# A segment mean on one core: looks in fewer operations, part of VectorE's work moved to GpSimd

## The chip, the cores and the metric

The kernel runs on one core of a Trainium2 chip. The metric is the device time of one execution in microseconds (us); lower is better. Each time below is the median of several executions, and the range stands beside it. The profile is one further execution, taken by the hardware profiler; its span is a little shorter than the times (193.8 us for the kernel before).

The engines: VectorE (DVE in the profile) and ScalarE (ACT) do the arithmetic, GpSimd (POOL) issues the gathers and does a little arithmetic, SyncE (SP) issues the plain loads, TensorE (PE) is hardly used. In the traces of this case each engine starts its instructions in the order in which the program records them, and stands still where something that it needs from another engine or from a DMA is not there yet (the stands below, of 6.5 and 8.4 us, are such waits).

## The reference

```python
n, num_segments = 10_000_000, 10000
data = randn(n) as float32
segment_ids = sorted random integers, int64

sums, counts = zeros(num_segments), zeros(num_segments)
np.add.at(sums, segment_ids, data)
np.add.at(counts, segment_ids, 1)
return sums / np.maximum(counts, 1)
```

The ids are sorted, and a segment has about 1000 elements. The kernel uses both facts, checks that they hold as it needs them, and has a slow general path for other inputs.

## The kernel before

Each of the 128 partitions holds 78,125 consecutive elements and goes through them in 98 rows of 800. A row of 800 is expected to hold at most one border between two segments. So the ids need not all be read:

1. *Probes.* Every 160th id is loaded. A **look** on VectorE (ten small operations for five rows) counts how many of a row's probes still equal the first one. This tells in which block of 160 the border lies.
2. *Gather.* GpSimd fetches the 159 ids at that place with an indirect DMA, one for each row.
3. *Id count.* ScalarE adds up the 159 gathered ids. VectorE turns the sums of five rows into border positions `KK` with one operation (`second_look`).
4. *Total and split.* ScalarE adds up the 800 data of the row. VectorE adds up those in front of the border, in one operation (`split`).
5. *Tables.* Now and then VectorE turns finished rows into segment counts, sums and means, puts them in order of the segments (`select`, `table`), and shifts each partition's table to its place in the output (`place`). A few checks add up flags that would call for the general path (`check`, `verdict`).

```python
def first_look(g):                       # before: 10 operations
    eq  = (probes == first probe)        # s1
    V   = first id of each row
    jc  = reduce(eq); BT = V[1:] - V     # s2
    ST  = jc * S + (1 + W)               # s3
    NB  = (BT != 1)
    pos = ST + wb                        # s4
    QQ  = V * W + ST
    IDX = NB * BIG + pos                 # s5
    QQ  = NB * (-64 * BIG) + QQ
    gather(g)                            # five indirect DMAs on GpSimd

def add_ids(r):
    nc.scalar.activation(
        out=junk_a[:, 0:W], in_=gt32[:, r % RING, 0 : 2 * W : 2], func=ACT.Relu,
        accum_out=GS[:, r : r + 1],
    )

def second_look(a, b):                   # KK = QQ - GS
    nc.vector.tensor_sub(out=KK[:, a:b], in0=QQ[:, a:b], in1=GS[:, a:b])

def split(r):                            # one operation per row on VectorE
    nc.vector.scalar_tensor_tensor(
        out=junk_v[:, 0:n], in0=iota[:, 0:n], scalar=KK[:, r : r + 1], in1=d,
        op0=ALU.is_lt, op1=ALU.mult, accum_out=A[:, r : r + 1],
    )
```

(These four are shortened; the first is in pseudo-code.) The author fixes the order of all instructions: the main loop goes row by row, and a list says which extra step is recorded behind which row. The engines' queues follow this order. The schedule of the tables before the change, with cuts:

```python
X_LOOK, X_SUM, RING = 11, 6, 28     # a look is 11 rows ahead, an id count 6 rows
for g in range(HEAD, NG):
    put(max(bounds[g] - X_LOOK, 0), first_look(g), 5)
put(45, select(0, 8, v))            # v: VectorE, g: GpSimd
put(52, sums(0, 48) + table(0, 8, v))
put(58, select(8, 12, v))
put(67, sums(48, 66) + table(8, 12, v) + place(0, 36, v), 2)
put(60, check(), 2)
# ...
for r in range(-X_PROBE - X_DATA, NR):
    # ... loads on SyncE, add_ids(r + X_SUM) on ScalarE ...
    total(r)                        # ScalarE
    split(r)                        # VectorE
    for f in after[r]:              # the steps put behind this row
        f()
```

## Time and profile before

The kernel before took 195.88 us (median of 3 runs, 195.34 to 196.23).

| engine | busy, share of the span | what it mainly does |
|---|---|---|
| VectorE | 148.1 us, 76% | 98 splits of 1.04 us, some 350 small operations (551 instructions less the splits and the reads of their sums) |
| ScalarE | 138.1 us, 71% | 98 totals of 0.87 us, 98 id counts of 0.35 us, and reading out the sums |
| GpSimd | 105.2 us, 54% | 98 gathers of 1.0 us |
| DMA | 9 tenths or more in 35 of 40 slices | 53 MB |

The page of the kernel before, part 1 (busy time, share of the span, instructions) and part 2 (busy tenths in 40 slices):

```profile
PE 1.6 (1%) x6; PEld 1.4 (1%) x6; DVE 148.1 (76%) x551; ACT 138.1 (71%) x393; POOL 105.2 (54%) x117
...
DVE  6438197868694958596788849997996778999991
ACT  0221789999987878595989679767949796977800
POOL 5487776764647383636456472757274564862000
DMA  6999999999999999999999999999999999993000
```

The DMA row is full up to slice 36, so the data stream sets the time up to about 177 us. Behind that VectorE alone stays at 9, up to slice 39: it finishes the last rows and tables. (A slice is 4.8 us.)

The groups of the kernel before (part 5 of the page: line, engine, operation, tiles, shapes, count, then busy us and mean ns, then the idle time in front and what ended most of it):

```profile
L289 POOL DMA_INDIRECT GT<-in_segment_ids_dram,IDX x98 | 98.3, 1003 | 66.7 <-ACT junk_a L299 26.0
L319 DVE SCALAR_TENSOR_TENSOR junk_v<-iota,q,data_t 128x800 bf16<-128x800 f32 x98 | 102.3, 1044 | 26.1 <-DMA data_t<-in_data_dram 24.6
...
L299 ACT ACTIVATE junk_a<-GT 128x159 bf16<-128x159 int32 x98 | 33.9, 346 | 23.6 <-DMA GT<-in_segment_ids_dram,IDX 19.5
```

VectorE's splits were idle for 26.1 us in all, of which data that had not landed ended 24.6 us. VectorE is faster than the stream and catches up with it again and again.

### The profile page before, as it was taken

Reading aid. Unit: us, or ns where it says so; the run is one execution under the profiler, and the core shown is the slowest. Engines: PE = TensorE matmul, PEld = TensorE weight load, DVE = VectorE, ACT = ScalarE, POOL = GpSimd, SP = SyncE. Lnnn points to the kernel's source line nnn. Section 1 sums busy time; section 2 is a strip of 40 time slices with the busy share of each in tenths; the row PEclk is TensorE's granted clock in tenths of the full one; section 3 lists DMA queues with packets and bytes.
Section 4 is the critical chain, followed back from the end, with each engine's and each line's share of the span. In section 5 each row is a group of like instructions: output and inputs, shape, how many; then the busy total and the mean of one; then the engine's idle time right before and its main releaser. Section 6 shows DMA issues by size and latency. Waiting matters only on the chain.

```text
span 193.8 us, 1611 instructions
## 1 busy us (share of the span) xinstructions
PE 1.6 (1%) x6; PEld 1.4 (1%) x6; DVE 148.1 (76%) x551; ACT 138.1 (71%) x393; POOL 105.2 (54%) x117
## 2 busy tenths in 40 slices
PE   0000000000000100000000000000000000001000
PEld 0000000000000100000000000000000000001000
DVE  6438197868694958596788849997996778999991
ACT  0221789999987878595989679767949796977800
POOL 5487776764647383636456472757274564862000
DMA  6999999999999999999999999999999999993000
GB/s 63 131 172 353 293 396 238 310 337 347 258 261 393 265 351 184 409 205 378 260 403 249 265 380 294 333 236 410 226 327 325 347 254 406 411 394 144 2 0 10
DMA packets 75141, 53.40 MB, mean 275 GB/s; under 512 B 65601, under 2 KB 65684, under 8 KB 75127
## 3 DMA queue, kind: packets, MB, share of 16 engines
q1 hardware_dynamic: 70251, 40.54, 74.6%
q0 software_dynamic: 4704, 12.74, 22.4%
q14 instruction: 14, 0.11, 0.2%
q10 hardware_dynamic: 172, 0.00, 0.1%
HBM read 56.46 MB, written 0.04 MB: 291 GB/s over the span
## 4 chain that ended last, share of the span: by engine, by line
DMA 37%; SPq 29%; issue 13%; DVE 13%; POOL 3%; ACT 2%; POOLq 0%; ACTq 0%; DVEq 0%
DMA data_t<-in_data_dram 31%; SPq L161 24%; DVE junk_v L319 6%; DMA GT<-in_segment_ids_dram,IDX 6%; SPq L153 5%; POOL GT L289 3%; ACT junk_a L314 1%; ACT junk_a L299 1%; DVE FF L572 1%; DVE most L706 0%; DVE add L701 0%; DVE pk L684 0%; DVE sel L628 0%; DVE sel L642 0%; DVE tab L647 0%
## 5 line engine op out<-in xcount | busy, mean ns | idle before, releaser
L289 POOL DMA_INDIRECT GT<-in_segment_ids_dram,IDX x98 | 98.3, 1003 | 66.7 <-ACT junk_a L299 26.0
L319 DVE SCALAR_TENSOR_TENSOR junk_v<-iota,q,data_t 128x800 bf16<-128x800 f32 x98 | 102.3, 1044 | 26.1 <-DMA data_t<-in_data_dram 24.6
L314 ACT ACTIVATE junk_a<-data_t 128x800 bf16<-128x800 f32 x98 | 85.0, 867 | 14.3 <-DMA data_t<-in_data_dram 11.6
L299 ACT ACTIVATE junk_a<-GT 128x159 bf16<-128x159 int32 x98 | 33.9, 346 | 23.6 <-DMA GT<-in_segment_ids_dram,IDX 19.5
L299 ACT ACTIVATION_READ_ACCUMULATOR junk_a<-GT 128x1 f32 x98 | 18.3, 186 | 0.0
L314 ACT ACTIVATION_READ_ACCUMULATOR junk_a<-data_t 128x1 f32 x98 | 18.3, 186 | 0.0
L306 DVE TENSOR_TENSOR q<-QQ,GS 128x5 f32<-128x5 f32 (+1 forms) x20 | 3.2, 160 | 8.2 <-ACT junk_a L299 8.2
L319 DVE DVE_READ_ACCUMULATOR junk_v<-iota,q,data_t 128x1 f32 x98 | 8.1, 83 | 0.0
L299 ACT ACT_TABLE_LOAD x1 | 1.3, 1283 | 7.7 <-DMA data_t<-in_data_dram 7.7
L245 DVE TENSOR_TENSOR eq<-pr 128x20 f32<-128x20 int32 (+1 forms) x20 | 3.5, 173 | 4.3 <-DMA pr<-in_segment_ids_dram 4.3
L254 DVE TENSOR_SCALAR ST<-jc 128x5 f32<-128x5 f32 (+1 forms) x20 | 3.7, 183 | 0.0
L250 DVE TENSOR_REDUCE jc<-eq 128x5 f32<-128x20 f32 (+1 forms) x20 | 3.5, 175 | 0.0
L258 DVE TENSOR_SCALAR NB<-q 128x5 f32<-128x5 f32 (+1 forms) x20 | 3.4, 168 | 0.0
L268 DVE TENSOR_TENSOR pos<-ST,wb 128x5 f32<-128x5 f32 (+1 forms) x20 | 3.3, 166 | 0.1
L275 DVE SCALAR_TENSOR_TENSOR IDX<-NB,pos 128x5 int32<-128x5 f32 (+1 forms) x20 | 3.3, 165 | 0.0
L247 DVE CAST q<-pr 128x6 f32<-128x6 int32 (+2 forms) x20 | 3.3, 164 | 0.0
L279 DVE SCALAR_TENSOR_TENSOR QQ<-NB,QQ 128x5 f32<-128x5 f32 (+1 forms) x20 | 3.2, 158 | 0.0
L269 DVE SCALAR_TENSOR_TENSOR QQ<-q,ST 128x5 f32<-128x5 f32 (+1 forms) x20 | 3.1, 157 | 0.0
L251 DVE TENSOR_TENSOR q<-q 128x5 f32<-128x5 f32 (+1 forms) x20 | 3.1, 155 | 0.0
L657 POOL TENSOR_TENSOR shf<-tab,dm 128x559 f32<-128x559 f32 x1 | 1.3, 1334 | 1.9 <-DVE tab L647 1.9
L647 DVE TENSOR_REDUCE tab<-sel 128x32 f32<-128x384 f32 (+2 forms) x3 | 1.6, 531 | 0.0
L170 DVE CAST wb<-wb_i 128x98 f32<-128x98 int32 x1 | 0.8, 783 | 1.1 <-POOL wb_i L169 1.1
(107 smaller groups left out, 41.8 us busy)
## 6 DMA issues: line engine op xcount, KB each, us to landing
data_t<-in_data_dram SPq DMA_DIRECT2D x48, 800.0 KB, 10.1
GT<-in_segment_ids_dram,IDX POOLq DMA_INDIRECT x98, 6.1
pr<-in_segment_ids_dram SPq DMA_DIRECT2D x18, 25.0 KB, 9.1
data_t<-in_data_dram SPq DMA_DIRECT2D x1, 400.0 KB
data_t<-in_data_dram SPq DMA_DIRECT2D x1, 262.5 KB, 16.7
out_dram<-OUT SPq DMA_DIRECT2D x1, 36.6 KB
pr<-in_segment_ids_dram SPq DMA_DIRECT2D x1, 21.0 KB
pr<-in_segment_ids_dram SPq DMA_DIRECT2D x1, 18.0 KB
```

Source lines behind the costliest of these rows:

```text
L153: nc.sync.dma_start(out=pr_flat[:, a:b], in_=ids_p[:, a * S : (b - 1) * S + 1 : S])
L161: nc.sync.dma_start(out=d[:, 0 : c - a], in_=data_p[:, a:c])
L245: nc.vector.tensor_tensor(out=eq, in0=in0b, in1=in1b, op=ALU.is_equal)
L247: nc.vector.tensor_copy(out=V[:, a:e], in_=pr32[:, a:e, 0])
L250: nc.vector.tensor_reduce(out=jc, in_=eq, axis=AX.X, op=ALU.add)
L254: nc.vector.tensor_scalar(out=ST[:, a:b], in0=jc, scalar1=float(S), scalar2=float(1 + W), op0=ALU.mult, op1=ALU.add,)
L258: nc.vector.tensor_scalar(out=NB[:, a:b], in0=BT[:, a:b], scalar1=1.0, scalar2=None, op0=ALU.not_equal)
L268: nc.vector.tensor_add(out=pos, in0=ST[:, a:b], in1=wb[:, a:b])
L289: nc.gpsimd.indirect_dma_start(out=GT[:, r % RING, :], out_offset=None, in_=ids2d[:], in_offset=bass.IndirectOffsetOnAxis(ap=IDX[:, r : r ...
L299: nc.scalar.activation(out=junk_a[:, 0:W], in_=gt32[:, r % RING, 0 : 2 * W : 2], func=ACT.Relu, accum_out=GS[:, r : r + 1],)
L314: nc.scalar.activation(out=junk_a[:, 0:n], in_=d, func=ACT.Copy, accum_out=t)
L319: nc.vector.scalar_tensor_tensor(out=junk_v[:, 0:n], in0=iota[:, 0:n], scalar=KK[:, r : r + 1], in1=d, op0=ALU.is_lt, op1=ALU.mult, accum_ ...
```

## The change

The intent: fewer operations on VectorE, which has no pause from 160.5 us to its end, and use of GpSimd, which is busy for 54% of the span only.

- A look takes seven operations instead of ten. The id count gets a bias of minus the row's first id for each partition, so that ScalarE's sum *is* the number of ids beyond the border, and less is left for VectorE to undo.
- Several table products, the window checks, and a new middle table move to GpSimd. The diff writes each fused operation of VectorE as two instructions of GpSimd, so a check becomes seven instructions there in place of four on VectorE.
- The counts take five steps instead of seven. Looks stand ten rows ahead instead of eleven, id counts five instead of six.

The core of the diff, with cuts:

```diff
-X_LOOK = 11
-X_SUM = 6
-RING = 28
+X_LOOK = 10
+X_SUM = 5
+RING = 20
...
     def add_ids(r):
         nc.scalar.activation(
             out=junk_a[:, 0:W], in_=gt32[:, r % RING, 0 : 2 * W : 2], func=ACT.Relu,
+            bias=NV[:, r : r + 1],
             accum_out=GS[:, r : r + 1],
         )
...
-            nc.vector.tensor_sub(out=KK[:, a:b], in0=QQ[:, a:b], in1=GS[:, a:b])
+            nc.vector.scalar_tensor_tensor(
+                out=KK[:, a:b], in0=JC[:, a:b], scalar=float(S), in1=GS[:, a:b], op0=ALU.mult, op1=ALU.subtract
+            )
...
     def windows_hold(r, n, o1, o2):
-        def s1():
-            nc.vector.scalar_tensor_tensor(
-                out=j1[:, 0:n], in0=KEY[:, PAD + r : PAD + r + n], scalar=-1.25, in1=ur[:, r : r + n],
-                op0=ALU.mult, op1=ALU.add,
-            )
+        e = nc.gpsimd
+        def s1():
+            e.tensor_scalar(
+                out=j1[:, 0:n], in0=KEY[:, PAD + r : PAD + r + n], scalar1=-1.25, scalar2=None, op0=ALU.mult
+            )
+            e.tensor_tensor(out=j1[:, 0:n], in0=j1[:, 0:n], in1=ur[:, r : r + n], op=ALU.add)
...
-    put(45, select(0, 8, v))
-    put(52, sums(0, 48) + table(0, 8, v))
-    put(58, select(8, 12, v))
-    put(67, sums(48, 66) + table(8, 12, v) + place(0, 36, v), 2)
+    put(43, select(M1, NT1 // 4, g))
+    t, p = table(M1, NT1 // 4, g, tax), place(CE, NO, tax, ...)
+    put(45, t[:1])                     # product on GpSimd
+    put(47, t[1:] + p[:1])             # its reduction on VectorE, then the place on GpSimd
+    put(44, select(0, 8, g))
+    put(58, select(8, 12, g))
+    t, p = table(8, 12, g, tab), place(0, 36, tab, ...)
+    put(69, t[:1])                     # product on GpSimd
+    put(71, t[1:] + p[:1])             # its reduction on VectorE
+    look = bounds[NG - 1] - X_LOOK
+    put(look + 3, verdict())
+    after[look + 6].append(lambda: verdict_reg.append(nc.values_load(...)))
```

The looks stand behind rows 44, 49, ... 64, 69, ..., five rows apart. So the products put behind rows 45 and 69 come into GpSimd's queue behind the five gathers of the look of row 44 or 69. (A product is one multiplication of a table's selection by the rows' means; VectorE then adds it up, its *reduction*.) These two places are what the study came to be about; they are called the first and the second **stand** below, because VectorE stands still there until GpSimd has the product.

## The prediction

> **What bounds the kernel now.** The timeline of SyncE shows its queue issuing back to back from 0.7 to 160.8 us, single data issues lasting 6 to 9 us[...]. The windows view gives a DMA share of 1.04 to 1.11 from 10 to 170 us. The last data lands at 177.1 us. Until then VectorE (76% busy) and ScalarE (71%) catch up again and again: VectorE waits 24.6 us for data in 16 waits (view of waits). So the stream sets the first 177 us, and the change moves none of its bytes. What can change is the tail: from 160.5 us VectorE runs without a pause, 16 splits at 1.09 us a row and about 12 us of small work, to 189.9 us; the output leaves and the span ends 3.9 us later.
>
> **What the change removes.** A look takes about 1.0 us now (ten operations, 0.1 us from start to start); seven save about 0.3 us in each of 20 groups, 6 us in all. Leaving VectorE: checks (some 16 operations, about 3 us), the equality and product of most tables (0.62 to 0.70 us for 528 elements), two counts operations per section. VectorE's busy time should fall from 148 to about 131 us. In the tail I count 3 to 3.5 us less VectorE work.
>
> **What it adds.** ScalarE: the count of ids gets a per-partition bias. The Trainium skill (ScalarE: Activation LUTs, "What ACT_TABLE_LOAD costs") puts a [128,1] pointer operand at about 93 ns; the trace has only the immediate form (346 ns), so as an estimate 98 x 0.093 = 9 us, from 1.46 to 1.55 us a row. The stream delivers a row in about 1.7 us, so this fits, with less slack.
>
> GpSimd: some 40 elementwise operations. In the trace 522 elements took 1.09 us (two inputs) and 1.55 us (compare with zero) there, against 0.70 us on VectorE; 18 elements took 0.36 us. Together about 20 us on top of gathers that hold GpSimd for 1.3 us each, 6.5 us a group.
>
> **Where I expect it to be given back.** GpSimd works in order. The order view shows the table products queued behind the five gathers of the look just before: product recorded after the looks of rows 44 and 69, their reductions on VectorE two to three rows later. VectorE is there after about 3.5 us, GpSimd after 7 to 9 us. So VectorE should stand still about 4 to 6 us near row 47 (98 us) and 4 to 7 us near row 71 (143 us), and again about 2 us for the verdict (row 87), whose last check waits behind the last four gathers and a placing product. The first loss is made up while the stream still runs (0.4 us a row); the second, only 20 us before the end of the stream, only in part. Later looks also delay gathers, and ScalarE with them.
>
> **Sum.** 195.9 - 3.3 (tail work) + about 2.5 (part of the second stall) + about 2 (verdict, later gathers) = 197.0 us; range 192.8 to 201.0. Faster by over 2%: 15%; within 2%: 57%; slower: 28%.
>
> **Right or wrong, by step.** Last data landing still near 177 us; VectorE busy near 131 us; id counts about 93 ns longer; in the view of waits, VectorE's table reductions waiting for GpSimd's products, over 3 us each, twice; bad-flag reduction waiting for GpSimd. If those waits are under 2 us, the kernel gains and ends near 192.5.
>
> **What would make it wrong.** Small GpSimd operations much faster or slower than those two samples (the sum moves about 1.3 us per 10% of them); VectorE's two-input operations held up by GpSimd's (FF took 0.92 instead of 0.18 us beside one); the stream ending elsewhere because gathers come later.

## The result, and the profile after

The changed kernel took 201.83 us (median of 4 runs, 201.75 to 202.15). The kernel before took 195.74 us in the same rounds (4 runs, 195.34 to 196.23). The ratio is 1.0313, with a 95% interval from 1.0286 to 1.034: slower by 3.1%. Here and below, a ratio is the mean time of one kernel's fast runs over that of the kernel before in the same rounds, so it is not quite the ratio of the medians.

The page of the changed kernel, the same parts:

```profile
PE 1.6 (1%) x6; PEld 1.4 (1%) x6; DVE 138.7 (69%) x470; ACT 147.1 (74%) x393; POOL 125.3 (63%) x161
...
DVE  6415396786876777879339967797408994939991
ACT  0052999999989999689786279997597549697930
POOL 5677745747557455476783776777773687789000
DMA  6999999999999999999999999999999999730000
...
L272 POOL DMA_INDIRECT GT<-in_segment_ids_dram,IDX x98 | 98.9, 1009 | 53.9 <-ACT junk_a L282 20.1
L305 DVE SCALAR_TENSOR_TENSOR junk_v<-iota,q,data_t 128x800 bf16<-128x800 f32 x98 | 101.8, 1039 | 9.6 <-DMA data_t<-in_data_dram 7.4
...
L282 ACT ACTIVATE junk_a<-GT,NV 128x159 bf16<-128x159 int32 x98 | 42.9, 438 | 28.5 <-DMA GT<-in_segment_ids_dram,IDX 23.4
```

VectorE has less to do (138.7 us instead of 148.1) and yet ends later. Its row shows two holes that were not there: "33" in slices 20 and 21 and "40" in slices 29 and 30 (a slice is 5 us). The stream is not longer: the DMA row falls off behind slice 34 (170 us) and not behind slice 36 (174 us). VectorE no longer waits much for data (7.4 us instead of 24.6): it has fallen behind the stream. The id count rose from 346 to 438 ns, by 92 ns. The Trainium skill (ScalarE: Activation LUTs, "What ACT_TABLE_LOAD costs") gives about 93 ns for a pointer operand of [128,1], and this trace agrees.

The view of waits of the changed kernel (engine, line and tile waiting, the releaser, then us in total, times, longest):

```profile
DVE q L290 <- ACT junk_a L282: 21.7, 10, 5.4
...
DVE tab L628 <- issue: 8.4, 1, 8.4
DVE junk_v L305 <- DMA data_t<-in_data_dram: 7.4, 5, 2.1
DVE tax L628 <- POOL sel L623: 6.5, 1, 6.5
...
DVE bad L499 <- POOL bad L428: 3.5, 1, 3.5
```

The first stand is the wait of `tax` (6.5 us), the second the wait of `tab` (8.4 us); the third is the verdict, waiting for the last check (3.5 us). For `tab` the profile names no releaser here, but the profile of a later kernel with the same two products (`e2_verdict`) does: `POOL sel L623`, 8.6 us.

The timelines of GpSimd and of VectorE in the changed kernel at the first stand (start us, us, engine, line, operation, tiles and shapes; in brackets the idle time before):

```profile
94.13 1.10 POOL L272 DMA_INDIRECT GT<-in_segment_ids_dram,IDX  x1 [1.45 <-ACT junk_a L300]
...
99.44 1.00 POOL L272 DMA_INDIRECT GT<-in_segment_ids_dram,IDX  x1 [0.30 <-issue]
100.47 0.87 POOL L611 TENSOR_TENSOR sel<-KEY,jj 128x384 f32<-128x384 f32 x1
101.42 1.18 POOL L612 TENSOR_SCALAR sel<-sel 128x384 f32<-128x384 f32 x1
102.58 0.74 POOL L623 TENSOR_TENSOR sel<-sel,RF 128x288 f32<-128x288 f32 x1
```

```profile
95.80 1.03 DVE L305 SCALAR_TENSOR_TENSOR junk_v<-iota,q,data_t 128x800 bf16<-128x800 f32 x1
...
103.35 0.45 DVE L628 TENSOR_REDUCE tax<-sel 128x24 f32<-128x288 f32 x1 [6.51 <-POOL sel L623]
```

GpSimd's own product takes 0.74 us. It starts at 102.58 us because five gathers (94.13 to 100.44 us) and an equality test in two instructions stand in front of it. VectorE, done with row 47 at 96.8 us, waits until 103.35 us.

At the second stand, GpSimd in the changed kernel:

```profile
143.81 1.11 POOL L272 DMA_INDIRECT GT<-in_segment_ids_dram,IDX  x1 [0.58 <-ACT junk_a L282]
...
149.14 0.99 POOL L272 DMA_INDIRECT GT<-in_segment_ids_dram,IDX  x1 [0.30 <-ACT junk_a L300]
150.16 0.58 POOL L623 TENSOR_TENSOR sel<-sel,RF 128x192 f32<-128x192 f32 x1
```

How far this carries is read from the time at which VectorE starts the split of a row (us from the span's start, from the traces; here and below differences are taken of the rounded times):

| row | before | after | difference |
|---|---|---|---|
| 45 | 94.4 | 93.3 | -1.1 |
| 48 | 100.0 | 104.3 | +4.3 |
| 69 | 138.5 | 138.3 | -0.2 |
| 72 | 143.4 | 151.0 | +7.6 |
| 84 | 164.0 | 169.7 | +5.7 |
| 96 | 185.4 | 191.4 | +6.0 |

Read alone, this table says that the first stand is made up by row 69 and that the loss is the second one's. The experiments show that this reading is wrong.

### The profile page after: what moved, and what is told of

The parts are those of the page before. It is cut to its first block, busy times and chain, and to the rows that moved or that the text cites. A ratio compares the mean times of both kernels' runs of the same rounds, so it can differ in the third digit from the quotient of the medians.

```text
span 200.0 us, 1589 instructions
## 1 busy us (share of the span) xinstructions
PE 1.6 (1%) x6; PEld 1.4 (1%) x6; DVE 138.7 (69%) x470; ACT 147.1 (74%) x393; POOL 125.3 (63%) x161
## 4 chain that ended last, share of the span: by engine, by line
SPq 29%; DMA 25%; issue 21%; ACT 8%; DVE 8%; POOL 7%; POOLq 0%; ACTq 0%
SPq L163 24%; DMA data_t<-in_data_dram 16%; DMA GT<-in_segment_ids_dram,IDX 9%; SPq L155 5%; POOL GT L272 4%; DVE junk_v L305 4%; ACT junk_a L282 4%; ACT junk_a L300 4%; POOL shf L638 1%; DVE q L290 0%; DVE most L691 0%; DVE add L686 0%; DVE pk L669 0%; POOL sel L611 0%; POOL j L437 0%
## 5 line engine op out<-in xcount | busy, mean ns | idle before, releaser
L282 ACT ACTIVATE junk_a<-GT,NV 128x159 bf16<-128x159 int32 x98 | 42.9, 438 | 28.5 <-DMA GT<-in_segment_ids_dram,IDX 23.4
L290 DVE SCALAR_TENSOR_TENSOR q<-JC,GS 128x5 f32<-128x5 f32 (+1 forms) x20 | 4.5, 223 | 23.3 <-ACT junk_a L282 21.7
L282 ACT ACTIVATION_READ_ACCUMULATOR junk_a<-GT,NV 128x1 f32 x98 | 18.3, 187 | 0.0
L282 ACT ACT_TABLE_LOAD x1 | 1.3, 1283 | 11.5 <-DVE NV L262 11.5
L612 POOL TENSOR_SCALAR sel<-sel 128x288 f32<-128x288 f32 (+3 forms) x4 | 3.7, 917 | 0.4
L250 DVE TENSOR_REDUCE JC<-eq 128x5 f32<-128x20 f32 (+1 forms) x20 | 3.5, 174 | 0.0
L251 DVE TENSOR_SCALAR far<-q 128x5 f32<-128x5 f32 (+1 forms) x20 | 3.5, 174 | 0.0
L259 DVE SCALAR_TENSOR_TENSOR pos<-JC,wb 128x5 f32<-128x5 f32 (+1 forms) x20 | 3.4, 172 | 0.0
L265 DVE TENSOR_TENSOR IDX<-pos,far 128x5 int32<-128x5 f32 (+1 forms) x20 | 3.4, 168 | 0.0
L262 DVE SCALAR_TENSOR_TENSOR NV<-far,pr 128x5 f32<-128x5 f32 (+1 forms) x20 | 3.3, 164 | 0.0
L249 DVE TENSOR_TENSOR q<-pr 128x5 f32<-128x5 int32 (+1 forms) x20 | 3.2, 160 | 0.0
```

Of the source, the lines that this page charges most:

```text
L250: nc.vector.tensor_reduce(out=JC[:, a:b], in_=eq, axis=AX.X, op=ALU.add)
L251: nc.vector.tensor_scalar(out=far, in0=BT[:, a:b], scalar1=1.0, scalar2=BIG, op0=ALU.not_equal, op1=ALU.mult)
L282: nc.scalar.activation(out=junk_a[:, 0:W], in_=gt32[:, r % RING, 0 : 2 * W : 2], func=ACT.Relu, bias=NV[:, r : r + 1], accum_out=GS[:, r : ...
L290: nc.vector.scalar_tensor_tensor(out=KK[:, a:b], in0=JC[:, a:b], scalar=float(S), in1=GS[:, a:b], op0=ALU.mult, op1=ALU.subtract)
L612: e.tensor_scalar(out=out, in0=out, scalar1=0.0, scalar2=None, op0=ALU.is_equal)
```

## The experiments

Eighteen kernels ran. In the tables "ratio" is against the kernel before in the same rounds.

### Is it the products' place in GpSimd's queue, and is it the verdict?

The theory: the loss comes from the products' place behind five gathers, and a smaller part from the verdict. Its rival: what costs is GpSimd's slower arithmetic, or ScalarE's longer id count. `e1_order` moves the two products in front of the gathers, and changes nothing else:

```diff
-    put(45, t[:1])
+    put(43, t[:1])
...
-    put(69, t[:1])
+    put(68, t[:1])
```

> The changed kernel with two lines moved: GpSimd forms the two table products (rows 45 and 69) just ahead of the next five gathers instead of just behind them; same work, same engines. Theory Q (VectorE stands still at the table reductions because GpSimd works in order and the products queue behind 6.5 us of gathers): the waits of 6.5 us at L628 tax and 8.4 us at L628 tab fall under 1 us each, and the time falls by 5 to 8 us from 201.8, to 194 to 197. Rival S (ScalarE is the cause: 9 us more busy from the bias, id counts late, VectorE waits 21.7 us for them): those waits stay at about 20 us and the time falls by less than 2 us, as the reductions merely wait elsewhere.

`e2_verdict` reads the verdict four rows later in the changed kernel; `e3_both` has both edits:

```diff
-    put(look + 3, verdict())
-    after[look + 6].append(...)
+    put(look + 7, verdict())
+    after[look + 10].append(...)
```

> The changed kernel with the verdict recorded four rows later (VectorE sums the bad flags after row 91 instead of row 87). Theory Q: the wait of 3.5 us at L499 for GpSimd's last check goes, on the path in the tail, so the time falls by 1 to 3 us to about 199 to 201. If the tail is bound by ScalarE instead (rival S), it stays within 0.5 us of 201.8.

> Both edits. Theory Q: the three waits of VectorE for GpSimd are gone, the saving of VectorE work in the tail comes through: 190.5 to 193.5 us, 1 to 3% faster than the kernel before. Rival S: still slower than the kernel before.

| kernel | median us | ratio (95%) | span of the profile |
|---|---|---|---|
| e1_order | 195.29 | 0.9965 (0.9891 to 1.0038) | 194.2 |
| e2_verdict | 201.14 | 1.0255 (1.0176 to 1.0334) | 199.5 |
| e3_both | 194.12 | 0.9904 (0.9825 to 0.9982) | 192.2 |

Four runs stand behind each median; the kernel before had 195.66 us in these rounds, and 195.74 us in those of the changed kernel, so the two may be set side by side. Moving two instructions by two rows and by one brings back 6.5 us (201.83 to 195.29). VectorE's wait for the first product is gone from the waits of `e1_order`, and of the second this is left:

```profile
DVE tab L628 <- POOL sel L623: 1.0, 1, 1.0
```

The medians put the verdict at 0.7 us beside the stands (201.83 to 201.14) and at 1.2 us without them (195.29 to 194.12), but the intervals of the ratios overlap in both pairs, so its size is not resolved. `e2_verdict` came out between its two expectations, and `e3_both` 0.6 us above its range. In the waits of `e3_both` both stands are gone:

```profile
DVE q L290 <- ACT junk_a L282: 20.5, 11, 5.3
DVE junk_v L305 <- DMA data_t<-in_data_dram: 15.5, 11, 3.2
...
DVE tab L628 <- POOL sel L623: 0.7, 1, 0.7
```

### Is it the place or the engine?

`h3_tables_dve` puts the two products back on VectorE in the rows that they have in the changed kernel:

```diff
-    t, p = table(M1, NT1 // 4, g, tax), place(...)
+    t, p = table(M1, NT1 // 4, v, tax), place(...)
...
-    t, p = table(8, 12, g, tab), place(...)
+    t, p = table(8, 12, v, tab), place(...)
```

> The changed kernel with the two table products back on VectorE, in the rows they have in the changed kernel; checks and middle stay on GpSimd. Theory (what costs is the place in GpSimd's queue behind five gathers, not GpSimd's own speed): 195 to 197 us, as in the run that only moved the products ahead of the gathers (195.3). Rival (GpSimd's own speed for the products costs too): 1 us or more below that run, 194.3 or less.

It took 195.43 us (4 runs), ratio 0.9923 (0.9841 to 1.0006). `e1_order` had 195.29 us, 0.9965. The two are alike within their intervals. So GpSimd's own time for the products costs nothing that these runs resolve; as far as they resolve it, all of the 6.5 us is the place in the queue.

### Which stand is the loss?

The theory, taken from the table of rows above and from the prediction: the first stand is made up, and the second is the loss. `h1_second` undoes the second stand alone (product from row 69 to row 68), `h2_first` the first alone (row 45 to row 43).

> The changed kernel with only the second table product (192 columns, row 69 of the stream) put one row earlier, ahead of the five gathers. Theory (the second stall is the one that is not made up, because too few rows are left after it): most of the 6 us come back, 195 to 197 us, ratio 0.995 to 1.006, and the wait of VectorE for the second product is gone from the list of waits while the first one stands at 6 to 8 us. Rival (both stalls count alike): 198 to 199 us.

> The changed kernel with only the first table product (row 45) put two rows earlier, ahead of the five gathers. Theory (the first stall is made up by the slack of the stream before row 69): less than 1.5 us is won, 200.5 to 202 us, ratio 1.024 to 1.032. Rival (both stalls count alike): 198 to 199 us.

| kernel | stands left | median us | ratio (95%) | span |
|---|---|---|---|---|
| changed kernel | both | 201.83 | 1.0313 (1.0286 to 1.034) | 200.0 |
| h1_second | first | 198.83 | 1.0112 (1.003 to 1.0194) | 196.6 |
| h2_first | second | 198.6 | 1.0111 (1.004 to 1.0183) | 196.5 |
| e1_order | none | 195.29 | 0.9965 (0.9891 to 1.0038) | 194.2 |

The theory falls and the rival stands: either stand alone is worth about 3 us, and together they make the 6.5. (By the ratios, which allow for the slower rounds of the h runs, it is about 2.9 us from `e1_order` to either, and 3.9 us from either to the changed kernel.) The waits of `h1_second`, then of `h2_first`, show that each has just the one stand left:

```profile
DVE tax L628 <- POOL sel L623: 6.5, 1, 6.5
...
DVE tab L628 <- POOL sel L623: 1.5, 1, 1.5
```

```profile
DVE tab L628 <- issue: 8.2, 1, 8.2
```

The rows tell why the first reading went astray (start of the split, us):

| row | e1_order | h1_second | lag of h1 | h2_first | lag of h2 |
|---|---|---|---|---|---|
| 48 | 99.8 | 104.5 | 4.7 | 98.2 | -1.6 |
| 69 | 136.8 | 138.4 | 1.6 | 134.9 | -1.9 |
| 72 | 142.9 | 144.2 | 1.3 | 147.5 | 4.6 |
| 84 | 163.3 | 165.9 | 2.6 | 165.7 | 2.4 |
| 96 | 185.4 | 188.0 | 2.6 | 187.9 | 2.5 |

The kernel before is the wrong yardstick for row 69: without the stand the changed kernel would have been there 1.7 us (138.5 to 136.8) *ahead* of it. (Each row time is from one profile, and the stream differs a little between profiles, as the lead of `h2_first` at row 69 shows; the medians do not rest on it.) Against that, the first stand still costs 1.6 us at row 69 and 2.6 us at the end. From row 48 to row 69 the lag falls by 3.1 us in 21 rows, 0.15 us a row on average. The prediction had 0.4 us a row.

The changed kernel and `h2_first` differ in the first stand alone, and up to row 47 their splits start within 0.5 us of each other. The stand puts the changed kernel 6.1 us behind at row 48. At row 52 it is 3.6 us, and from there the lag does not shrink: 3.4 us at row 69, 3.5 us at row 97. Of the 2.5 us gained in these four rows some 1.7 us are not catching up: two operations of the look behind row 49 are held up in `h2_first` while GpSimd computes (1.62 and 0.44 us, against 0.18 and 0.16 us in the changed kernel). From row 53 to row 69 VectorE has about 5.5 us of waits in both, but in `h2_first` 5.0 us of them are for data, and in the changed kernel all are for id counts, this one first:

```profile
121.42 0.35 DVE L290 SCALAR_TENSOR_TENSOR q<-JC,GS 128x5 f32<-128x5 f32 x1 [3.36 <-ACT junk_a L282]
```

The idle time that should have made up the lag went to id counts that were late too.

### Is the lag kept in the gathers?

In `h1_second` the gathers from row 59 on are issued 2 to 3 us later than in `e1_order`, up to the last, and ScalarE waits more for them after 100 us (11.4 us against 5.1). In the changed kernel they are issued 3.5 to 3.9 us later than in `h2_first`, also up to the last. This suggested a loop: the stand delays VectorE's looks, these delay the gathers, these delay the id counts, and these VectorE. `i1_ahead` therefore gives the looks five more rows of lead in the changed kernel, with the verdict left in its row; `i2_ahead_order` does the same in `e1_order`:

```diff
-X_LOOK = 10
+X_LOOK = 15
...
-    look = bounds[NG - 1] - X_LOOK
+    look = bounds[NG - 1] - 10
```

> The changed kernel with the looks (and so the gathers) five rows further ahead of their use, X_LOOK 15 instead of 10; looks still stand in rows 44 and 69, so each table product still stands behind five gathers, and VectorE still waits for it 6 to 8 us twice. Theory (a stand of VectorE delays the looks, so the gathers, so the id counts of ScalarE, and the lag is kept there): with five more rows of lead the late gathers do no harm, ScalarE's waits for gathered ids after 100 us (17.9 us in the changed kernel) fall below 6 us, and the time falls by 2 to 4 us, to 198 to 200 us. Rival (VectorE's own work after the stands keeps the lag): 201 us or more.

> The same with both table products moved ahead of the gathers, as in the run that gave 195.3 us. Its distance to the run before it is what the two stands cost when gathers have five more rows of lead. Theory: 2 to 4 us instead of 6.2 us (so 195 to 196.5 us here). Rival: 6 us as before, so about 195 us here with 201 us there.

`i1_ahead` took 200.2 us (4 runs), ratio 1.0222 (1.0166 to 1.0278); `i2_ahead_order` took 192.88 us (4 runs), ratio 0.9842 (0.9788 to 0.9897). The distance is 7.3 us and not 2 to 4; `i1_ahead` lies between its two expectations, and `i2_ahead_order` below both of its own. ScalarE's waits for gathered ids after 100 us did fall, from 17.9 to 4.5 us (with another 4.5 us that the profile puts down to VectorE's `IDX`), but the time fell by only 1.6 us (201.83 to 200.2). The waits of VectorE in `i1_ahead`:

```profile
DVE tab L628 <- POOL sel L623: 14.6, 2, 10.9
...
DVE tax L628 <- POOL sel L623: 6.5, 1, 6.5
...
DVE junk_v L305 <- DMA data_t<-in_data_dram: 0.7, 2, 0.5
```

The list covers the whole run, and what is left out lies before 85 us, but for 4.3 us. From 85 us to the end VectorE waits in this run for almost nothing but products (21.1 us) and one set of probes (4.3 us), and works in all other time. In this run the lag is kept in VectorE's own work. The test is not quite clean, since the second stand grew (10.9 us against 8.4; the other 3.7 of the 14.6 us are a wait for a third product at 127 us, which `i2_ahead_order` has too, 3.5 us). But the lag left by row 69 points the same way: against `i2_ahead_order` it is 6.7 us at row 48 and 2.5 us at row 69, so 0.2 us a row were made up, and again some 1.7 us of that are operations of `i2_ahead_order` held up beside GpSimd. So more lead takes the waits for id counts away and the lag still stays for the most part. In the changed kernel both are at work, the late id counts and VectorE's own work, and these runs do not say how much is due to each. What a faster recovery would need is idle time of VectorE: in `e1_order` it is busy for 31.5 of the 38 us from 100 to 138 us, so 17% is the most that can be idle, 0.3 us of a row of about 1.75 us. That is a bound worked out from busy time; waits and the gaps between instructions take part of it.

`i2_ahead_order` is also 1.2% under `e1_order`, and has no wait of ScalarE for gathered ids after 100 us. With the stands moved away (waits of 3.5 and 2.9 us for products are left), more lead for the gathers seems to help; the two intervals just touch.

### What the bias costs

`e4_bias` adds to the kernel before a bias of zeros, so that the id counts take longer and nothing else changes; it needs a small tile for the zeros. `f1_nobias` takes the bias out of `e3_both`, so its result is wrong.

```diff
+    nul = cpool.tile([P, 1], FP32, name="nul")
+    nc.vector.memset(nul, 0.0)
...
+            bias=nul[:, 0:1],
```

> The kernel before with one thing added: the count of ids takes its bias (zero) from a 128x1 tile. Theory Q: the id counts go from 346 to about 438 ns, ScalarE's busy time from 138 to 147 us, and the time stays within 1 us of the kernel before, because ScalarE has room under the stream of data. Rival S: 2 us or more slower.

> e3_both without the bias operand, its result wrong on purpose[...]. It tells what ScalarE's bias costs inside the changed kernel. If it matters (ScalarE at 1.55 us a row in the tail makes VectorE wait 2.8 us for id counts after 160 us there, 20.5 us in all), the waits at L290 fall below 12 us and the time drops 1 to 3 us below e3_both, a ratio of 0.975 to 0.985 to the kernel before. If ScalarE has room, as the prediction had it, the ratio stays at 0.99 within 0.004.

`e4_bias` came out *faster*: 192.59 us (5 runs), ratio 0.9822 (0.9749 to 0.9895). `f1_nobias` took 193.84 us, 0.9926 (0.9862 to 0.999), against 0.9904 of `e3_both`: the 98 times 92 ns, 9 us of ScalarE, cost nothing that can be measured in that schedule. (VectorE's waits for id counts were 16.5 us there, not under 12; its splits, which read the wrong values, took 1041 ns, and 1040 ns in `e3_both`.) A surprise of 1.8% had to be followed up, since it could have put every other comparison in doubt. `f3_bias_again` is the same kernel with more rounds:

> The same kernel as e4_bias (the kernel before plus a bias pointer of zeros), repeated because four of its five executions were 2 to 3 us faster than the kernel before while the profiled one was not, which neither theory foretold. If that is real, the ratio is again 0.975 to 0.99; if it was chance, 0.997 to 1.005.

192.56 us (6 runs), ratio 0.9862 (0.9811 to 0.9914). So it is real. The zero tile, however, also moves all later tiles by 32 bytes. In the built programs the data tiles start at byte 56,544 of a partition before (96 modulo 128) and at byte 56,576 (0 modulo 128) with the extra tile. `g1_pad` moves the tiles alone, `g2_bias_nopad` has the bias alone (a column of zeros that is there already), `h4_pad96` puts the data at 64 modulo 128:

```diff
+    pad = cpool.tile([P, 8], FP32, name="pad")     # g1_pad; [P, 24] in h4_pad96
+    nc.vector.memset(pad, 0.0)
```

```diff
+            bias=PX[:, 0:1],                         # g2_bias_nopad
```

> The kernel before with one unused tile of 32 bytes a partition put ahead of the data tiles; no bias. In the build of the kernel before, the data tiles start at byte 56544 of a partition (32 past a multiple of 64); in the run with the bias pointer, whose added tile shifted them, and in the changed kernel they start at a multiple of 64. Theory P (place in SBUF: the stream of data runs faster into tiles at a multiple of 64): ratio 0.98 to 0.99 and the last data lands near 173 us. Theory B (the bias operand does it): ratio 0.997 to 1.003.

> The kernel before with the bias pointer read from a column of zeros that is there anyway, so no tile moves. Theory P: ratio 0.997 to 1.005 (ScalarE has room for 9 us). Theory B: 0.98 to 0.99, as in f3_bias_again.

> The kernel before with 96 unused bytes ahead of the data tiles, which then start at 64 mod 128 instead of 96 mod 128. If only a start at a multiple of 128 bytes makes the difference seen with 32 bytes (ratio 0.993): ratio 1.000 within 0.003. If a multiple of 64 is enough: ratio 0.993 within 0.003.

The place was tried on another kernel too: `f2_checks_dve` (below; 64 modulo 128) with 32 and 64 bytes in front.

> f2_checks_dve with its data tiles moved by 32 bytes, so that they lie as in the kernel before. Theory P: 1 to 2% slower than f2_checks_dve, ratio to the kernel before 0.995 to 1.005, and then the change, even with its waits mended, saves nothing by its work. If the place does not matter: ratio 0.986 within 0.004.

> f2_checks_dve with its data tiles moved by 64 bytes, to a multiple of 128 instead of 64. Control for g3_f2_pad32: if only the multiple of 64 matters, ratio 0.986 within 0.004; if 128 matters, 0.975 to 0.982, and it beats both kernels.

| kernel | data start mod 128 | median us | ratio (95%) |
|---|---|---|---|
| before, in the rounds of the two g runs on it | 96 | 196.78 | 1 |
| g2_bias_nopad | 96 | 196.18 | 0.9959 (0.9908 to 1.001) |
| g1_pad | 0 | 195.14 | 0.9931 (0.9889 to 0.9973) |
| f3_bias_again (bias and move) | 0 | 192.56 | 0.9862 (0.9811 to 0.9914) |
| h4_pad96 | 64 | 196.15 | 0.9959 (0.99 to 1.0018) |
| f2_checks_dve | 64 | 192.89 | 0.9857 (0.981 to 0.9904) |
| g3_f2_pad32 | 96 | 193.93 | 0.9863 (0.9818 to 0.9908) |
| g4_f2_pad64 | 0 | 192.03 | 0.9789 (0.9747 to 0.9831) |

(The kernel before took 196.13 us beside `f2` and `f3`, 196.78 us beside the four g runs and 196.53 us beside `h4`; so compare ratios.) A start at a multiple of 128 bytes goes with about 0.7% less time twice (before to `g1_pad`, and `f2`/`g3` to `g4`, whose intervals overlap); `g1_pad` lies between its two theories. 96 and 64 are alike in the second kernel; `h4_pad96` lies between and its interval holds both answers, so whether 64 is worth anything to the kernel before stays open. The mechanism stays open as well, and so does why bias and move together give 1.4% when one alone gives 0.7% and the other nothing certain. It is enough that the kernels before and after have their data at 96 and 64 modulo 128, and `e1`, `e2`, `e3`, `h1`, `h2`, `h3` and `i1`, `i2` all at the place of the changed kernel: the place of the data is not what tells them apart.

### What else is on GpSimd, and the lead of the id counts

`f2_checks_dve` takes `e3_both` and puts the window checks and one `select` back on VectorE; `f4_sum6` gives the id counts of `e3_both` six rows of lead instead of five.

```diff
-        e = nc.gpsimd                    # in windows_hold and single, called from check
+        e = nc.vector
...
-    put(77, select(12, M1, g))
+    put(77, select(12, M1, v))
```

```diff
-X_SUM = 5
+X_SUM = 6
```

> e3_both with the window checks of rows 0 to 82 and the last selection (240 elements) put back on VectorE, where they fall in rows in which it waits for data. GpSimd loses some 6 us of work between gathers. If the work on GpSimd delays gathers and so ScalarE and the id counts in the tail: 0.5 to 2 us faster than e3_both, ratio 0.98 to 0.987. If VectorE has no room for it: slower than e3_both, ratio above 0.993.

> e3_both with ids counted one row earlier on ScalarE (look-ahead of 6 rows as in the kernel before, instead of 5), which gives VectorE's split points 1.5 us more slack but ScalarE 1.5 us less for a gather to land. If VectorE's 20.5 us of waits for id counts come from the shorter look-ahead, they fall below 12 us and the ratio to 0.98; if they come from late gathers, ScalarE only waits earlier, and the ratio stays at 0.99 within 0.005.

`f2_checks_dve` took 192.89 us (6 runs), ratio 0.9857 against 0.9904 of `e3_both` (other rounds, and the intervals overlap): more work on VectorE and less on GpSimd was no loss, and perhaps a gain of 0.5%. `f4_sum6` took 194.6 us, 0.9915 (0.9852 to 0.9977): no effect, and 16.9 us of waits for id counts, not under 12. With 64 bytes of padding, `f2_checks_dve` is `g4_f2_pad64`, 192.03 us: 2.1% faster than the kernel before (1.7 to 2.5%) and the best of all that ran. `i2_ahead_order`, at 1.6%, suggests that the longer lead of the looks is worth having too; the two were not tried together.

## Why the prediction was wrong

The prediction was 197.0 us, with a range up to 201.0; it was 201.83 us. Its mechanism was right, and so were the two places where it would bite. Two terms of its sum had the wrong size, a third erred the other way.

**Right.** *What bounds the kernel before* and that the stream would not change: the DMA row ends about 4 us earlier, not later. *The id count*: 92 ns more where 93 were said, and it costs nothing measurable (`f1_nobias`). *The look*: in the timelines it takes 0.98 us before (101.09 to 102.07) and 0.69 us after (92.57 to 93.26), so 0.3 us saved. *The waits*: "VectorE's table reductions waiting for GpSimd's products, over 3 us each, twice", at 98 and 143 us, and the "bad-flag reduction". These waits began at 96.8, 142.4 and 176.1 us.

**Wrong: "The first loss is made up while the stream still runs (0.4 us a row)".** This is the step that failed. The row table of `h1_second` gives 0.15 us a row on average, the rows of `i1_ahead` 0.2 us; and in the changed kernel, set against `h2_first`, nothing at all was made up after row 52 (3.6 us there, 3.5 us at row 97), while VectorE's idle time, 5.5 us up to row 69, went to waits for late id counts. (That these waits keep the lag is read from the traces; no edit shows it, since `i1_ahead` took them away and yet kept most of its lag.) The stand took 6.5 us, within the expected "4 to 6" but for half a us, and about 3 us of it were still there at the end. It stood in the sum with nothing. The prediction did say that "later looks also delay gathers, and ScalarE with them", but it did not see that this takes away the idle time on which its 0.4 us a row rested.

**The second stand** took 8.4 us where "4 to 7" were said, and cost about 3 us (`h2_first` and the changed kernel against `e1_order`), near the 2.5 us in the sum. The two stands together measured 6.5 us against 2.5 in the sum: 4 of the 4.8 us by which the prediction missed.

**The tail, "195.9 - 3.3".** With the stands and the verdict out of the way, `e3_both` is 1.5 us faster than the kernel before (195.66 to 194.12), so the tail gave about half. Its timeline shows where some of it went: VectorE waits 2.1 us for the id counts of its last groups.

```profile
172.39 0.40 DVE L290 SCALAR_TENSOR_TENSOR q<-JC,GS 128x5 f32<-128x5 f32 x1 [2.14 <-ACT junk_a L282]
```

In `i2_ahead_order`, where the gathers come earlier and VectorE has no such wait, the gain is 3.0 us (195.88 to 192.88). So most of the 3.3 us may have been there, behind gathers that came too late for it. That this is the whole reason is argued from these two runs, and not shown by an edit of that wait alone.

**The verdict, "about 2"**, measured 0.7 us with the stands and 1.2 us without, neither of them resolved. It erred in the other direction, by about 1 us.

So the prediction's sum -3.3 + 2.5 + 2 should have read -1.5 + 6.5 + 1.2. (That these give about 201.8 us from the 195.66 us of those rounds is no check of them: each is a difference between two neighbours in the row from the kernel before to `e3_both`, `e1_order` and the changed kernel.)

**VectorE's busy time near 131 us** was wrong too: 138.7 us. The instructions fell from 551 to 470, but most of these were small ones that overlap: they last 0.16 us but start 0.08 to 0.12 us apart, and 81 fewer took 9.4 us away, 0.12 us each. Some of those left take longer when GpSimd computes beside them, which the prediction named as a danger. As an estimate from the timelines after 30 us, such hold-ups add up to 0.7 us before and 1.7 us in the changed kernel, so they are about 1 us of the 7.7 by which it missed; the rest is not accounted for. (In `e3_both` they come to about 5.8 us; what they cost there was not tested.) Two instructions of VectorE beside one of GpSimd, in the timelines of the kernel before and of `e3_both`:

```profile
170.19 1.09 POOL L630 TENSOR_TENSOR pk<-KL,jj 128x522 f32<-128x522 f32 x1
...
170.40 0.92 DVE L572 TENSOR_TENSOR FF<-q,CS 128x18 f32<-128x18 f32 x1
```

```profile
177.28 1.29 POOL L666 TENSOR_TENSOR pk<-pk,BM 128x570 f32<-128x570 f32 x1
...
177.88 0.70 DVE L502 TENSOR_TENSOR bads<-bad 128x1 f32<-128x1 f32 x1
```

Both small operations end within 0.04 us of GpSimd's; another such `FF` of 18 elements at 187.06 us, alone, takes 0.18 us. The Trainium skill (SBUF — State Buffer, "SBUF: two separate sides") says that GpSimd and a VectorE operation with two SBUF inputs share a pair of ports under an exclusive lock, for the whole instruction. This trace agrees that the small operation is held until GpSimd's is done. The section gives the ports to whichever of the two starts first; by the recorded starts, which are rough for GpSimd, this is not always so here. In `e3_both` an operation that starts 0.6 us before GpSimd's, which runs from 147.64 to 148.79 us, was held as well, and ends 0.02 us after it:

```profile
147.04 1.77 DVE L265 TENSOR_TENSOR IDX<-pos,far 128x5 int32<-128x5 f32 x1
```

## What to carry to other kernels

When work moves to an engine that also issues DMAs, ask what stands in front of it in that engine's queue: here two products of 0.7 and 0.6 us made VectorE wait 6.5 and 8.4 us, because five gathers stood in front of each, and recording them two rows and one row earlier gave back 3% of the kernel. Judge whether a stall is made up against the same kernel without the stall, and not against the kernel before: a part of the change that gains can hide a stall that still costs. Work out the recovery from the idle time of the engine that is late, and not from the distance between its best pace and the stream's; and ask whether that idle time is still idle when the work that the engine feeds to others comes late as well.

## What the Trainium skill lacked or had wrong

- GPSIMD Engine Reference, "When to use GPSIMD": it says that gathers are GpSimd's work and that it makes the descriptors, but that section has no number for how long a gather keeps GpSimd's queue. Here a gather of 159 ids for each of 128 partitions takes 1.0 us, and 0.3 us pass until the next, so five hold back arithmetic behind them by 6.5 us.
- GPSIMD Engine Reference, "Engine selection": an elementwise operation with one input is said to run at roughly line rate, and one with two inputs at about half the speed of VectorE. Here the compare of one input with zero, 128x384, took 1.18 us on GpSimd, and the test of two inputs of that size 0.87 us; VectorE took 0.55 us for two inputs (so the two-input ratio is 1.6, and the one-input operation is the slower one; so it is with a multiplication by a constant, 128x68: 0.39 us, against 0.33 us for the sum of two inputs).
- SBUF — State Buffer, "Operand start alignment": only the element size is asked for, and the section says that its runs timed nothing. Here a start of the data tiles at a multiple of 128 bytes went with 0.7% less time in two kernels (0.9931, and 0.9857 or 0.9863 to 0.9789, where the intervals overlap); the mechanism is not known.
- ScalarE: Activation LUTs, "What ACT_TABLE_LOAD costs": nothing to mend. The cost of a pointer operand (93 ns) was met within 1 ns, and so was the table load's time (1283 ns in the trace).
